# Scaling the third tile's finished rows in the last output stage, and splitting the last weight quarter three products sooner

## The chip, the core and the metric

The kernel runs on one NeuronCore of a Trainium2 chip. The metric is the device time of one execution in microseconds (us); a median over runs is given where there are several. Five engines appear in the profile: PE (TensorE, matrix products, with PEld for its weight loads), DVE (VectorE), ACT (ScalarE), POOL (GpSimd) and SP (SyncE, which here only issues DMAs). Each takes its own instructions strictly in the order in which they stand in the program, and waits where an instruction needs a result of another engine.

## The reference

Two layers on a residual stream x of 2048 rows by 1024 columns: a gated MLP with chunk-wise mixing, then attention of 64-row chunks to themselves and the 8 chunks before, with one key and value projection for all. What matters here is the end of it:

```python
def rms_norm(x, g):
    xf = x.astype(jnp.float32)
    y = xf * lax.rsqrt(jnp.mean(xf * xf, axis=-1, keepdims=True) + EPS)
    return (y * g.astype(jnp.float32)).astype(x.dtype)

def chunk_attention_mixer(h, k_pad, v_pad, w_qz, rel_bias, w_out):
    ...
    o = lax.map(one_chunk, (jnp.arange(n_chunks), q))      # softmax(q k + bias) v, 16 heads of 64
    return (o * jax.nn.silu(z)) @ w_out

x = x + chunk_attention_mixer(h, k_pad, v_pad, b_w_qz[i], b_rel_bias[i], b_w_out[i])
return rms_norm(x, final_norm_g)
```

## The kernel before

The attention layer works on four tiles of 512 rows (t = 0 to 3; the third tile is t = 2), and within a tile on eight pairs of heads (p = 0 to 7). A pair has eight score steps (two heads, four blocks of 128 queries). Beside these steps PE is given products of other work: the projections of the next pair, and the output projection of the tile before. In the last pair, t = 3 and p = 7, there is no next pair; there the rest of tile 2's output projection and the first 13 steps of tile 3's own stand beside the scores. What is left of tile 3's projection follows alone, and is called the last output stage here.

**Products.** Every product is taken in float32 accuracy by splitting both factors into a high and a low part of a faster type. The high part is a copy on ACT (L356 for the left factor, L1775 for a weight), the low part a subtraction on DVE (L361 `Qlo<-A_hh,Qho`, L1776 `wbo<-raw_bo,wbo`). Three matmuls (L111, L112, L113) multiply high by high, high by low, low by high; only the third needs the left factor's low part, only the second the weight's.

**The output projection** is one level of Strassen: seven products `ph` in the order 1, 7, 2, 6, 5, 4, 3, each for two halves `jp` of the rows. A product (ph, jp) is 4 groups of three matmuls, 12 in all. `last_all` (L1796) lists them for tile 3: `ltodo` holds the 14 pairs, so i = 5 is (2, 1), i = 7 is (6, 1) and i = 8 is (5, 0). In the second group of product i it splits the left factor of product i + 2 (`last_left`), and a table `plan` says which weights are fetched there (`last_right`). The weights of ph 1, 2 and 3 are plain quarters of the matrix that are fetched raw and split; the others were stored split. The quarter of ph 3, the last one, is fetched and split at i = 5.

**Evictions.** `o_evict` (L1819) adds each product into the rows: DVE reads PSUM and adds (L1927, L1932, L1941, L1949), POOL adds two tiles of SBUF (L1929, L1937, L1942, L1945). The first two products are copied by ACT. When a 128-row block is complete, ACT squares it (L1861) into a sum `ssq`, and `finish` (L1878) adds the two halves of the sum on DVE (L1881), adds epsilon (L125), takes the root on POOL (L126, 128x1), and `scale` multiplies the row by the root and the gain on DVE: two SCALAR_TENSOR_TENSOR of 128x512 at L1899. For tile 3 that comes at once. For tile 2 the finished sums go to DRAM (`x2d`), and `finish` fetches them back into a tile `y`, scales and sends them out.

**When tile 2's rows are finished.** The four `finish` calls of tile 2 (blocks 1, 3, 0, 2 in that order) are put on a list `finals`, each puts its `scale` in front of it, and something pops one entry at a time. Up to now two places do: the loop over the eight score steps (`if u and finals`, one entry per step), in the last pair as elsewhere, and `last_all`, once per product after i = 4. So blocks 1, 3 and 0 are scaled in the last pair, and block 2 in the last output stage.

**What sets the order.** The kernel is written in this order, and a planner of the tile framework then fixes one order per engine, from its own estimates and from tiles' data dependencies. `on_tick`, `on_beat` and `follow` add edges to that: an instruction may not be placed ahead of a named matmul (`tick`, `beat`) or instruction. Those edges set the order on one engine and cost no wait on the chip. A DMA is queued on SP in the order given; one that must wait, for its data or for a free buffer, holds all behind it.

## Time and profile before

| what | us |
|---|---|
| median of 3 runs (lowest and highest) | 2638.99 (2638.98 to 2643.34) |
| the profiled execution, its whole time | 2639.15 |
| its span, first to last instruction | 2637.2 |
| PE busy in the span | 2603.7 |
| DVE busy in the span | 1874.3 |
| POOL busy in the span | 884.6 |

Rows of a timeline hold the start, the duration, engine, line and operation with output and inputs, how many (x1), and in brackets the idle time of the engine just before with what ended it. Where several stand in one row (x2), the duration is that of all. A duration includes time in which the instruction, already issued, stands still; the next one often starts a little before it ends (0.60 us from start to start for a DVE row of 0.68). The view by stretches gives for each stretch the busy time of PE, PEld, DVE, ACT and POOL with the number of instructions, the granted PE clock as a share, the DMA engines' share and GB/s. The view of waits names who waited, for whom, the sum in us, how often, and the longest.

### The profile page before, as it was taken

To read this page: it belongs to the slowest core of one execution; us is meant where nothing else is said; L and a number is where in the kernel's file an instruction comes from. 1 tells how busy PE (TensorE), PEld (TensorE's weight loads), DVE (VectorE), ACT (ScalarE), POOL (GpSimd) and SP (SyncE) were. 2 spreads that over 40 slices of the span, in tenths; PEclk is the share of its full clock that TensorE was granted. 3 is DMA by queue.
4 is the path that set the end of the run, shared out by engine and by line. 5 is a ranking of instruction groups with operands and counts; after the bars stand their busy time and mean duration, and the time that the engine had idled before them with its cause. 6 is when DMAs were issued, how large, how long until landed. Compare 5 with 4: busy or idle time off the path is not lost. (4 is left out here: it accounts for less than half of the span.)

```text
span 2637.2 us, 38020 instructions
## 1 busy us (share of the span) xinstructions
PE 2603.7 (99%) x12976; PEld 2178.5 (83%) x12976; DVE 1874.3 (71%) x2942; ACT 1314.5 (50%) x2331; POOL 884.6 (34%) x871
## 2 busy tenths in 40 slices
PE   9999999999999999999999999999999999999997
PEld 7888888888888888888888878888888888888886
DVE  6655676866767667757776767777778777877677
ACT  5422243443433434343376566666656655666564
POOL 4611334143152322203233334344332322332245
PEclk9999999999999999999999999999999999999999
DMA  7899999999988869967886587778787666775677
GB/s 297 317 344 331 346 365 318 320 326 337 336 298 309 316 232 323 333 203 266 317 287 223 190 273 237 227 244 260 245 279 259 221 210 219 254 228 160 195 228 250
DMA packets 275153, 720.31 MB, mean 273 GB/s; under 512 B 28944, under 2 KB 68880, under 8 KB 274960
## 3 DMA queue, kind: packets, MB, share of 16 engines
q1 hardware_dynamic: 268096, 704.25, 77.8%
q10 hardware_dynamic: 6864, 13.63, 1.4%
q8 instruction: 104, 1.70, 0.3%
q14 instruction: 89, 0.73, 0.1%
HBM read 532.69 MB, written 174.59 MB: 268 GB/s over the span
## 5 line engine op out<-in xcount | busy, mean ns | idle before, releaser
L111 PE MATMUL P<-T,S 128*128 128x512 f32 x1248 | 495.1, 397 | 0.1
L113 PE MATMUL P<-T,S 128*128 128x512 f32 x1248 | 487.7, 391 | 0.0
L112 PE MATMUL P<-T,S 128*128 128x512 f32 x1248 | 487.3, 390 | 0.0
L1560 POOL TENSOR_SCALAR pr<-pr,sl 128x640 f32<-128x640 f32 (+4 forms) x256 | 205.9, 805 | 555.3 <-DVE sl L1559 469.0
L111 PE MATMUL pj<-hh_b,wh_b 128*128 128x512 f32 x768 | 319.0, 415 | 0.0
L113 PE MATMUL pj<-hh_b,wl_b 128*128 128x512 f32 x768 | 303.9, 396 | 0.3 <-DVE wl_b L242 0.3
L112 PE MATMUL pj<-hl_b,wh_b 128*128 128x512 f32 x768 | 302.3, 394 | 0.0
L1556 ACT ACTIVATE pr<-pr,nm 128x640 f32<-128x640 f32 (+4 forms) x256 | 195.5, 764 | 188.9 <-DVE nm L1549 187.2
L113 PEld LDWEIGHTS P<-T,S 128*128 128x128 f32 x1248 | 234.3, 188 | 50.7 <-DVE S L463 0.4
L112 PEld LDWEIGHTS P<-T,S 128*128 128x128 f32 x1248 | 235.0, 188 | 44.8 <-DVE T L463 0.5
L111 PEld LDWEIGHTS P<-T,S 128*128 128x128 f32 x1248 | 234.8, 188 | 44.9 <-DVE x L596 0.5
L1581 DVE TENSOR_TENSOR pt<-tp,pt 128x640 fp32r<-128x640 f32 (+4 forms) x256 | 188.6, 737 | 44.2 <-ACT pt L1580 41.5
L1549 DVE CUSTOM_DVE_ANT_0 pr<-s,bias 128x640 f32<-128x640 f32 (+4 forms) x256 | 188.1, 735 | 36.3 <-PE s L1541 29.8
L1580 ACT CAST pt<-tp 128x640 fp32r<-128x640 f32 (+4 forms) x256 | 158.7, 620 | 52.6 <-PE tp L1576 47.5
L1576 PE MATMUL tp<-ident,pr 128*128 128x128 f32 x1120 | 166.7, 275 | 11.0 <-DVE pt L1581 10.3
L113 PEld LDWEIGHTS pj<-hh_b,wl_b 128*128 128x128 f32 x768 | 144.2, 188 | 34.7 <-DVE wl_b L242 2.3
L1576 PEld LDWEIGHTS tp<-ident,pr 128*128 128x128 f32 x1120 | 130.7, 140 | 46.0 <-issue 15.4
L111 PEld LDWEIGHTS pj<-hh_b,wh_b 128*128 128x128 f32 x768 | 145.1, 189 | 17.4 <-ACT wh_b L241 1.2
L112 PEld LDWEIGHTS pj<-hl_b,wh_b 128*128 128x128 f32 x768 | 145.1, 189 | 16.6
L1601 PEld LDWEIGHTS pv<-pt,V 128*128 128x128 f32 x896 | 143.1, 188 | 18.4 <-DVE pt L1581 2.3
L1601 PE MATMUL pv<-pt,V 128*128 128x256 f32 (+3 forms) x896 | 153.8, 319 | 0.4 <-DVE pt L1581 0.4
L242 DVE TENSOR_TENSOR wl_b<-raw_b,wh_b 128x1024 fp32r<-128x1024 f32 x96 | 120.4, 1255 | 25.7 <-ACT wh_b L241 24.7
(307 smaller groups left out, 5723.6 us busy)
## 6 DMA issues: line engine op xcount, KB each, us to landing
S<-hsd SPq DMA_DIRECT2D x288, 512.0 KB, 5.5
rw<-in_w_a SPq DMA_DIRECT2D x108, 512.0 KB, 6.4
raw_b<-wk SPq DMA_DIRECT2D x75, 512.0 KB, 4.3
A<-ytd SPq DMA_DIRECT2D x72, 512.0 KB, 5.8
hsd<-S SPq DMA_DIRECT2D x56, 512.0 KB, 4.7
V<-vhd SPq DMA_DIRECT2D x56, 512.0 KB, 5.6
bias<-reld SPq DMA_DIRECT2D x64, 320.0 KB, 4.1
va<-vd SPq DMA_DIRECT2D x32, 512.0 KB, 6.0
```

The lines of the kernel that those rows point to most:

```text
L111: first = mm(ps, lh, rh, start=first, stop=False)
L112: mm(ps, lh, rl, start=False, stop=False)
L113: mm(ps, ll, rh, start=False, stop=last)
L242: tv(wl[:], raw[:], wh[:].bitcast(F32), op=sub)
L1549: nc.vector.tensor_tensor_reduce(out=pr[:, c0:].rearrange("p (a b) -> p a b", a=nseg), in0=ps[:, :nseg, :w], in1=bias[:, c0:].rearrange("p ...
L1556: nc.scalar.activation(pr[:, c0:], pr[:, c0:], AF.Exp, scale=-1.0, bias=nm[:], accum_out=sl[:])
L1560: nc.gpsimd.tensor_scalar(pr[:, c0:], pr[:, c0:], sl[:], 1.0, op0=ALU.mult, op1=ALU.mult)
L1576: ins = tpose(tp[:, b, :], pr[:, b * P : (b + 1) * P], ident[:])
L1580: nc.scalar.copy(oh, tp[:, b0:5, :].rearrange("p a b -> p (a b)"))
L1581: nc.vector.tensor_tensor(pt[:, 2560 + o + b0 * P : 2560 + o + 640], tp[:, b0:5, :].rearrange("p a b -> p (a b)"), oh.bitcast(F32), op=ALU ...
L1601: mm(po[:, q0 * P : q1 * P], vtl[t, p][:, i, hs], rhs, start=(i == blocks[0] and j == 0), stop=(i == 7 and j == 1),)
```

## The change

Four edits, all at the end of tile 3.

- The pops of `finals` by the score loop stop in the last pair (`t + 1 < NT or p + 1 < NPAIR`). In `last_all` they come in every second group of three matmuls (k = 1 and 3) after i = 4, in place of once per product. So all four blocks of tile 2 are finished and scaled in the last output stage: an entry at each of the eight places from (2, 1) to (6, 1) and (5, 0).
- Block 3 (b = 3) gets its own tile of two halves (tag C) in place of sharing the one tile `y` of tag bx with blocks 1 and 2.
- The fetch of the last weight quarter (ph = 3) stays listed at i = 5, while its split becomes a function `halves` that is listed at i = 7 for its first half and i = 8 for its second. A new argument `late` of `split_s` makes the left factor's split of (4, 0) follow the weight's, on ACT and on DVE, and the weight's split may not be placed ahead of the matmul named last (`on_tick`).
- Nothing is added to or left out of the arithmetic.

```diff
             ins = nc.scalar.copy(hi[:, ks], src[:, ks])
...
-            tv(lo[:, ks], src[:, ks], hi[:, ks].bitcast(F32), op=sub)
+            follow(ins, late[::2])
+            follow(tv(lo[:, ks], src[:, ks], hi[:, ks].bitcast(F32), op=sub), late[1::2])
...
+                late=late_w if (ph, jp) == (4, 0) else (),
...
-                nc.scalar.copy(w[0], raw[:])
-                tv(w[1], raw[:], w[0].bitcast(F32), op=sub)
+                def halves():
+                    hi = nc.scalar.copy(w[0], raw[:])
+                    lo = tv(w[1], raw[:], w[0].bitcast(F32), op=sub)
+                    if ph == 3:
+                        late_w.extend((on_tick(hi).ins.name, lo.ins.name))
+                if ph == 3:
+                    late_s.append(halves)
+                else:
+                    halves()
...
-                        if finals and i > 4:
-                            finals.pop(0)()
+                    if closed and i > 4 and k % 2 and finals:
+                        finals.pop(0)()
...
+                        if i in (7, 8):
+                            late_s.pop(0)()
...
-                elif t + 2 == NT and b == 0:
+                elif t + 2 == NT and b in (0, 3):
                     on_beat(first)
-                    y = [half_tile("og", f"y{t}_{b}_{c}", 2)[:] for c in range(2)]
+                    tag, n = ("C", 4) if b else ("og", 2)
+                    y = [half_tile(tag, f"y{t}_{b}_{c}", n)[:] for c in range(2)]
...
-                    if u and finals:
+                    if u and finals and (t + 1 < NT or p + 1 < NPAIR):
                         finals.pop(0)()
```

Nothing moves on any engine before the last pair. How the planner's order changes is shown at three places. In the names, `y2_3_0` is tile 2's row block 3, its first half; `Qlo_5_1` is the low part of the left factor of product (5, 1); `bo_6_0` is product (6, 0) in PSUM; `row1` and `ou3` are the rows and partial sums of tile 3; `pt3_15`, `pr3_15` and `s3_15` belong to the scores of head 15.

The first place is DVE in the middle of the last pair, at the last head's blocks. Before, from the split of (7, 0) on:

```order
L361 TENSOR_TENSOR Qlo_7_0_25429<-A_hl_25181,Qho_7_0_25428 128x512
L1621 TENSOR_TENSOR og32_3_7_25458<-pv3_14_25432,ot3_14_25459 64x512
L1581 TENSOR_TENSOR pt3_15_25449<-tp3_15_0_25450,pt3_15_25449 128x640
L1899 SCALAR_TENSOR_TENSOR y2_3_25375<-y2_3_25375,rr_f2_3_25371,gf_13667 128x512 x2
L1549 ISA pr3_15_3_25474,nm3_15_3_25475<-s3_15_3_25469,bias3_15_25125 128x640
L1549 ISA nm3_15_3_25475 128x1
L1581 TENSOR_TENSOR pt3_15_25449<-tp3_15_1_25490,pt3_15_25449 128x640
L1881 TENSOR_TENSOR rr_f2_0_25502<-ssq2_0_23968 128x1
L361 TENSOR_TENSOR Qlo_7_1_25520<-A_hl_25181,Qho_7_1_25519 128x512
L1559 RECIPROCAL sl3_15_3_25476<-sl3_15_3_25476 128x1
L125 TENSOR_SCALAR rr_f2_0_25502<-rr_f2_0_25502 128x1
L1899 SCALAR_TENSOR_TENSOR y2_0_0_25506<-y2_0_0_25506,rr_f2_0_25502,gf_13667 128x512
```

Now, from the same split on:

```order
L362 TENSOR_TENSOR Qlo_7_0_25411<-A_hl_25181,Qho_7_0_25410 128x512
L1622 TENSOR_TENSOR og32_3_7_25440<-pv3_14_25414,ot3_14_25441 64x512
L1550 ISA pr3_15_3_25456,nm3_15_3_25457<-s3_15_3_25451,bias3_15_25125 128x640
L1550 ISA nm3_15_3_25457 128x1
L1582 TENSOR_TENSOR pt3_15_25431<-tp3_15_0_25432,pt3_15_25431 128x640
L1560 RECIPROCAL sl3_15_3_25458<-sl3_15_3_25458 128x1
L362 TENSOR_TENSOR Qlo_7_1_25492<-A_hl_25181,Qho_7_1_25491 128x512
L1582 TENSOR_TENSOR pt3_15_25431<-tp3_15_1_25472,pt3_15_25431 128x640
L1781 TENSOR_TENSOR wlbo_2_1_25405<-raw_bo_2_1_25406,whbo_2_1_25404 128x1024
```

The scalings of blocks 3 and 0 and the small steps of their roots are gone from between the score steps; those of block 1, a little earlier, are gone as well.

The second place is DVE in the last output stage, at products (6, 0) to (4, 0). Before, from the eviction of (6, 0) on:

```order
L1941 TENSOR_TENSOR ou3_1_0_25484<-bo_6_0_25704,ou3_1_0_25484 128x512
L361 TENSOR_TENSOR Qlo_5_1_25734<-A_hl_25181,Qho_5_1_25733 128x512
L1941 TENSOR_TENSOR ou3_1_1_25529<-bo_6_1_25726,ou3_1_1_25529 128x512
L361 TENSOR_TENSOR Qlo_4_0_25754<-A_hh_25180,Qho_4_0_25753 128x512
L1927 TENSOR_TENSOR row1_25625<-bo_5_0_25746,row1_25625 128x512
L1932 TENSOR_TENSOR ou3_1_0_25484<-bo_5_0_25746,ou3_1_0_25484 128x512
L361 TENSOR_TENSOR Qlo_4_1_25778<-A_hh_25180,Qho_4_1_25777 128x512
```

Now, from the same eviction to the split of (4, 0):

```order
L1956 TENSOR_TENSOR ou3_1_0_25466<-bo_6_0_25668,ou3_1_0_25466 128x512
L1781 TENSOR_TENSOR wbo_3_0_25646<-raw_bo_3_0_25647,wbo_3_0_25646 128x1024
L362 TENSOR_TENSOR Qlo_5_1_25720<-A_hl_25181,Qho_5_1_25719 128x512
L1914 SCALAR_TENSOR_TENSOR y2_0_0_25713<-y2_0_0_25713,rr_f2_0_25709,gf_13667 128x512
L1956 TENSOR_TENSOR ou3_1_1_25501<-bo_6_1_25700,ou3_1_1_25501 128x512
L1914 SCALAR_TENSOR_TENSOR y2_3_0_25681<-y2_3_0_25681,rr_f2_3_25677,gf_13667 128x512
L1895 TENSOR_TENSOR rr_f2_2_25743<-ssq2_2_24023 128x1
L1914 SCALAR_TENSOR_TENSOR y2_3_1_25682<-y2_3_1_25682,rr_f2_3_25677,gf_13667 128x512
L125 TENSOR_SCALAR rr_f2_2_25743<-rr_f2_2_25743 128x1
L1781 TENSOR_TENSOR wbo_3_0_25646<-raw_bo_3_1_25649,wbo_3_0_25646 128x1024
L1914 SCALAR_TENSOR_TENSOR y2_0_1_25714<-y2_0_1_25714,rr_f2_0_25709,gf_13667 128x512
L362 TENSOR_TENSOR Qlo_4_0_25752<-A_hh_25180,Qho_4_0_25751 128x512
```

Six operations of two SBUF tiles now stand ahead of the low part of (4, 0): both halves of the weight split, and four halves of rows. After it come the eviction of (5, 0), the two halves of block 2 and `ou3_1_0`, and then `Qlo_4_1`. Block 1 takes the place that block 2 had, right behind `Qlo_6_1`.

The third place is POOL in the same stretch. Before, its sums follow each other:

```order
L1929 TENSOR_TENSOR row2_25558<-row2_25558,ou3_1_1_25529 128x512
L1942 TENSOR_TENSOR ou3_7_0_25586<-ou3_7_0_25586,ou3_1_0_25484 128x512
L1945 TENSOR_TENSOR row1_25625<-row1_25625,ou3_7_0_25586 128x512
L1937 TENSOR_TENSOR ou3_7_0_25586<-ou3_7_0_25586,row1_25625 128x512
L1942 TENSOR_TENSOR ou3_7_1_25639<-ou3_7_1_25639,ou3_1_1_25529 128x512
```

Now the roots of blocks 3 and 0 stand ahead of them:

```order
L1944 TENSOR_TENSOR row2_25528<-row2_25528,ou3_1_1_25501 128x512
L126 TENSOR_TENSOR rr_f2_3_25677<-rr_f2_3_25677,mhalf_179 128x1
L126 TENSOR_TENSOR rr_f2_0_25709<-rr_f2_0_25709,mhalf_179 128x1
L1957 TENSOR_TENSOR ou3_7_0_25548<-ou3_7_0_25548,ou3_1_0_25466 128x512
L1960 TENSOR_TENSOR row1_25587<-row1_25587,ou3_7_0_25548 128x512
L1952 TENSOR_TENSOR ou3_7_0_25548<-ou3_7_0_25548,row1_25587 128x512
L1957 TENSOR_TENSOR ou3_7_1_25601<-ou3_7_1_25601,ou3_1_1_25501 128x512
L1960 TENSOR_TENSOR row3_25589<-row3_25589,ou3_7_1_25601 128x512
L1952 TENSOR_TENSOR ou3_7_1_25601<-ou3_7_1_25601,row3_25589 128x512
L126 TENSOR_TENSOR rr_f2_2_25743<-rr_f2_2_25743,mhalf_179 128x1
```

The last two of its sums, `ou3_1_0` and `ou3_1_1`, follow there as before. On ACT both casts of the weight quarter now stand right behind the square of `row2` (product (2, 1)); the high part of (5, 1) lies between them and those of (4, 0) and (4, 1) follow. PE's order changes by a few places: among them, the first matmul of (4, 1) is placed ahead of the third of (4, 0), and the first of (3, 0) ahead of the third of (4, 1). On SP the fetches and stores of `y` for blocks 1, 3, 0 and 2 that stood between the weight fetches now stand behind the last of them, except the fetch of block 1.

## Prediction

> **What bounds the kernel now.** I read the page's busy shares first, then busy time by stretches over the end, then PE's waits there, then the timelines of DVE, POOL and PE. Nothing moves ahead of the last pair, so only the last 65 us count. From the page, and from the stretches (PE, PEld, DVE, ACT, POOL, the clock, the DMA share, GB/s) of the last pair and of the first part of the last output stage:

> ```profile
> PE 2603.7 (99%) x12976; PEld 2178.5 (83%) x12976; DVE 1874.3 (71%) x2942; ACT 1314.5 (50%) x2331; POOL 884.6 (34%) x871
> ```

> ```profile
> 2575.00:2598.00 23.00, 20.21 (x111) 16.46 (x110) 19.50 (x35) 13.18 (x25) 11.29 (x11) 1.00 0.91 306
> 2598.00:2620.00 22.00, 22.00 (x99) 18.18 (x98) 15.48 (x24) 9.53 (x21) 16.20 (x12) 1.00 0.74 283
> ```

> PE is the bound nearly everywhere, but in the last pair it stands for 2.8 us while DVE is busy 19.5 of 23 us. In the output stage PE never stands, DVE has 6.5 us to spare and POOL 5.8. Those two look free there; whether they are, the rest decides. PE's waits from 2574 to 2624, as a view gives them:

> ```profile
> PE tp L1576 <- DVE pt L1581: 2.4, 3, 1.1
> PE bo L112 <- DVE wbo L1776: 1.3, 2, 0.7
> PE s L1541 <- DVE nm L1549: 0.7, 1, 0.7
> PE tp L1576 <- DVE rr_f L1881: 0.3, 1, 0.3
> ```

> 2.4 + 0.7 + 0.3 = 3.4 us are score steps waiting for DVE in the last pair; 1.3 us is product (3, 0) waiting twice for the low half of its weight.

> **A. The scalings leave the last pair.** DVE's rows there:

> ```profile
> 2574.57 2.56 DVE L1899 SCALAR_TENSOR_TENSOR y<-y,rr_f,gf 128x512 f32<-128x512 f32 x2
> ...
> 2585.55 1.88 DVE L1899 SCALAR_TENSOR_TENSOR y<-y,rr_f,gf 128x512 f32<-128x512 f32 x2
> ...
> 2591.18 0.75 DVE L1899 SCALAR_TENSOR_TENSOR y<-y,rr_f,gf 128x512 f32<-128x512 f32 x1 [1.48 <-POOL rr_f L126]
> ...
> 2595.06 0.74 DVE L1899 SCALAR_TENSOR_TENSOR y<-y,rr_f,gf 128x512 f32<-128x512 f32 x1
> ```

> 2.56 + 1.88 + 0.75 + 0.74 = 5.9 us of DVE and 1.48 us of standing for POOL's root go. That is more than PE's 3.4 us of waits. I leave 0.6 of them, about one eviction, since an eviction and splits still stand between the score steps: **−2.8**, which is also what PE lacks in the stretch (23.00 − 20.21). Ends: −3.4 if all goes, −1.4 if only what the idle 1.48 us caused goes.

> **B. The weight's split comes sooner.** Around product (3, 0), and at the anchors that I need below, PE's rows are:

> ```profile
> 2612.48 0.39 PE L111 MATMUL bo<-wbo,Qho 128*128 128x512 f32 x1
> ...
> 2615.20 0.39 PE L111 MATMUL bo<-whbo,Qho 128*128 128x512 f32 x1
> ...
> 2620.64 0.39 PE L111 MATMUL bo<-wbo,Qho 128*128 128x512 f32 x1
> 2621.71 0.50 PE L112 MATMUL bo<-wbo,Qho 128*128 128x512 f32 x1 [0.69 <-DVE wbo L1776]
> ...
> 2627.69 0.39 PE L113 MATMUL bo<-wbo,Qlo 128*128 128x512 f32 x1
> ```

> Products (5, 1) and (4, 0) start 2.72 us apart, so a matmul takes 0.227. From 2620.64 to 2621.71 pass 1.07, so this wait cost 0.84 where the view says 0.69; 1.3 × 0.84 / 0.69 = 1.6. The split is now placed ahead of that of (4, 0), so **−1.6**. The last matmul, without these waits, would end at 2627.69 + 0.23 − 1.58 = 2626.34 (all times on the axis of before, A taken apart).

> **C. What the last stage now carries.** Six operations of two SBUF tiles stand on DVE ahead of the low part of (4, 0): two weight halves, four row halves. On POOL two roots come ahead of the sum of (6, 0). Whether DVE and POOL can do this side by side is seen where such operations meet. First POOL, then DVE (the last two fences start with the same instruction, alone and with its successor):

> ```profile
> 2609.45 1.30 POOL L1942 TENSOR_TENSOR ou<-ou,ou 128x512 f32<-128x512 f32 x1
> 2610.82 1.81 POOL L1945 TENSOR_TENSOR row<-row,ou 128x512 f32<-128x512 f32 x1
> ...
> 2618.82 1.75 POOL L1937 TENSOR_TENSOR ou<-ou,row 128x512 f32<-128x512 f32 x1
> 2620.54 2.27 POOL L1937 TENSOR_TENSOR ou<-ou,row 128x512 f32<-128x512 f32 x1
> ```

> ```profile
> 2611.40 0.68 DVE L1941 TENSOR_TENSOR ou<-bo,ou 128x512 f32<-128x512 f32 x1
> 2612.00 1.18 DVE L361 TENSOR_TENSOR Qlo<-A_hh,Qho 128x512 fp32r<-128x512 f32 x1
> ```

> ```profile
> 2619.95 1.71 DVE L1776 TENSOR_TENSOR wbo<-raw_bo,wbo 128x1024 fp32r<-128x1024 f32 x1
> ```

> ```profile
> 2619.95 3.94 DVE L1776 TENSOR_TENSOR wbo<-raw_bo,wbo 128x1024 fp32r<-128x1024 f32 x2
> ```

> They do not run together. POOL's second sum ends at 2620.57, the first weight half at 2621.66 (1.09 later), POOL's third sum at 2622.81 (1.15 later), the second weight half at 2623.89 (1.08 later). So they take strict turns, also where DVE has its next operation waiting, and hold 1.09 per weight half and 1.15 per sum. A low part beside a sum: 2613.18 − 2612.63 = 0.55; I take 0.57 for it and for a row half. The eviction at 2611.40, which reads PSUM, goes on in its 0.60 while the sum from 2610.82 runs.

> Now the turns. In before the sum of (6, 0) starts at 2609.45; two roots, 0.5 each (the stretch from 2632 below has one of 0.55), put it to 2610.45. From there to the end of the low part of (4, 0): POOL six sums, 6.9, and block 2's root, 0.5; DVE two weight halves, 2.2, and six operations of 0.57, 3.4; and the eviction of (6, 1), 0.6, in which POOL has nothing ready, as its next sum needs just that. 6.9 + 0.5 + 2.2 + 3.4 + 0.6 = 13.6, so 2624.05. The low part of (5, 1) is third behind the first weight half: 2610.45 + 1.15 + 1.15 + 1.09 + 1.15 + 0.57 = 2615.56.

> PE needs the latter at its third matmul, 2612.48 + 0.45 = 2612.93: a wait of **2.6**. (4, 0) then starts at 2617.8, and three matmuls later, at 2618.5, PE stands until 2624.05: **5.55**. The low part of (4, 1) follows an eviction, block 2's two halves and one more eviction: 2624.05 + 0.6 + 1.14 + 0.6 + 0.57 = 2626.96, where PE is ready at 2626.77: 0.2 (one matmul of (4, 1) was drawn ahead of the long wait). Behind it 33 matmuls are left, 7.5 us: last end 2634.45, against 2626.34: **+8.1**.

> Two inputs could make this worse. The cast of the first weight half on ACT stands behind the square of (2, 1)'s rows, and the quarter must have landed:

> ```profile
> 2609.52 0.63 ACT L1861 ACTIVATE jk<-row 128x512 f32<-128x512 f32 x1 [2.33 <-POOL row L1929]
> ```

> ```profile
> L1775 ACT CAST wbo<-raw_bo x2: 1032/1042/1052, 2618.9 to 2619.8; 128x1024 fp32r<-128x1024 f32 x2
> ```

> ```profile
> 2599.88 0.32 SPq L1779 DMA_DIRECT2D wlbo<-ows  x1
> ...
> 2602.46 1.61 SPq L1774 DMA_DIRECT2D raw_bo<-in_wb_out  x2
> ```

> ```profile
> raw_bo<-in_wb_out SPq DMA_DIRECT2D x2, 512.0 KB, 11.1
> ```

> The first half's fetch now stands where the row at 2599.88 stood; with 11.1 us it lands at 2611.0 and is cast by 2612.05, before its turn at 2612.75: no cost. Issued at 2602.46 as before, it would be cast at 2614.65; a sum of 1.15 would fill part of the gap, and 0.8 would remain. The fetches of blocks 3 and 0 now stand behind the weights and the store of block 1 on SP; if DVE has to wait for them, a sum on POOL takes its turn meanwhile, so I cost them at nothing.

> **The clock.** In the tail the granted clock shows what a long wait does:

> ```profile
> 2631.00:2632.00 1.00, 0.00 (x0) 0.00 (x0) 0.97 (x4) 0.18 (x2) 0.00 (x0) 0.89 0.08 29
> 2632.00:2633.00 1.00, 0.00 (x0) 0.00 (x0) 0.34 (x2) 0.00 (x0) 0.55 (x1) 0.50 0.99 365
> ```

> A mean of 0.89 means a fall to 0.50 at 2631.78, 3.7 us after the last matmul. In a wait from 2618.5 it would fall at 2622.2. No row shows when it returns. If after another 3.7 us, at 2625.9, then 1.85 us of work run at half: I take **+0.9**; ends 0 (the fall comes later) and 1.85 (3.7 us of work at half). [...]

> **D. The tail.** Its last scaling starts in before at

> ```profile
> 2632.76 1.41 DVE L1899 SCALAR_TENSOR_TENSOR row<-row,rr_f,gf 128x512 f32<-128x512 f32 x2 [0.66 <-POOL rr_f L126]
> ```

> and ends 6.25 us after the last matmul. The same chain hangs on (3, 1) afterwards: **0**.

> **The sum.** A −2.8, then +6.5 for the last matmul (C's 8.1 less B's 1.6), clock +0.9, D 0: +4.6. The profiled execution took 2639.15 (its span 2637.2), so 2643.75; the median of the runs is 0.16 lower: **2643.6**. No change means within 0.2%, 5.3 us, about what a measurement of this kernel can tell.

> **The rivals.** *The clock comes back late.* Half rate for 3.7 us of work costs 1.85, for two such stretches 3.7; the sum without the clock is +3.7, so +5.5 to +7.4, **2644.5 to 2646.4**: slower. It decides from the point where the wait is longer than 3.7 us and the clock still stands at 0.50 two microseconds after PE resumes. For it: the fall in the tail, and a wait of 5.55. Against: the fall may come late in the wait, and a shorter wait avoids it. Chance 0.25. [...]

> *DVE takes turn after turn* while it has work, and POOL comes in only where DVE does something else. The first weight half goes at 2612.75; DVE's own work from there to the low part of (4, 0) is 2.2 + 3.4 + 0.6 = 6.2, and two sums come in, at the eviction and at the tiny steps of a root: 2612.75 + 6.2 + 2.3 = 2621.25. The low part of (5, 1) is there at 2614.4. The waits are 1.5, 3.9 and, with a sum ahead of the low part of (4, 1), 1.3; less the matmul drawn ahead, 0.2, +6.5, and −4.4 + 6.5 = +2.1, with hardly a fall of the clock: **2641.1**. Against: the two weight halves with a sum between them. Chance 0.13.

> *The quarter lands late.* The first half of it costs 0.8 more, as above: **2644.4**. For it: 11.1 us from issue to landing, and only 0.7 in hand. Against: its place on SP. Chance 0.12.

> *The stage hides it.* If DVE's 6.5 us of spare time were all usable, as the shares suggest, C would be near 0: −2.8 − 1.6 = −4.4, **2634.6**. Against: every row above in which one of the two waits. Chance 0.06.

> *It does not do what it says*: the order shows the moved instructions; 0.01, 2638.8.

> **How the numbers follow.** Forecast 0.43, late clock 0.25, turn after turn 0.13, late quarter 0.12, hidden 0.06, nothing 0.01. The range leaves out the last two at its lower end, 2639.0, and reaches at its upper from 2646.4 by A's near end (+1.4) to 2648.0. Slower begins at 2644.3: most of the late clock (0.22), half of the late quarter (0.06), a quarter of the forecast (0.11): 0.39. Faster, below 2633.7, needs the hidden case with A at its far end, and a little more: 0.03. The rest, 0.58, is no change.

> **What would show it.** A: no wait of tp or s for DVE in the last pair. B: no wait for `wbo`. C: PE waits at L113 for `Qlo` in (5, 1) and (4, 0), together about 8 us, with DVE and POOL rows lengthened beside each other in turns; wrong if these waits stay below 4. Clock: a stretch at 0.50 inside the wait. The prediction falls if PE stays busy through (4, 0), or if the tail behind the last matmul changes by over a microsecond.

## The result and the profile after

| kernel | median, us | lowest to highest | runs |
|---|---|---|---|
| before | 2640.62 | 2636.32 to 2643.34 | 9 |
| changed | 2646.55 | 2643.81 to 2648.55 | 9 |

The ratio is 1.0021, with a 95% interval of 1.0012 to 1.0030: about 5.5 us slower, between 3.2 and 7.9. The interval leaves out a ratio of 1, so the kernel is slower; but the ratio stands on the bound of 0.2%, and whether the true one is over it, these runs leave open. The profiled execution took 2646.11 us, its span is 2643.9 (before 2639.15 and 2637.2). The forecast was 2643.6 and +4.6.

Executions differ by some microseconds before anything moved, so the stages are measured from one row of the last pair but one, ahead of all that the change touches (in the twelve profiles it starts between 2539.67 and 2544.57). It stands 1.43 us later in the profile of the changed kernel, and that much of the two spans' difference is not the change. Before, then after:

```profile
2540.21 2.66 PE L1601 MATMUL pv<-pt,V 128*128 128x512 f32 x16
```

```profile
2541.64 2.65 PE L1602 MATMUL pv<-pt,V 128*128 128x512 f32 x16
```

Product (5, 0) starts before the change at

```profile
2609.76 0.39 PE L111 MATMUL bo<-wbo,Qho 128*128 128x512 f32 x1
```

| from that row, us | to product (5, 0) | (5, 0) to the last matmul | last matmul to the last scaling | all |
|---|---|---|---|---|
| before | 69.55 | 17.93 | 5.07 | 92.55 |
| changed | 66.85 | 26.08 | 4.84 | 97.77 |
| difference | −2.70 | +8.15 | −0.23 | +5.22 |

The last scaling after the change, on DVE, is this:

```profile
2639.41 1.42 DVE L1914 SCALAR_TENSOR_TENSOR row<-row,rr_f,gf 128x512 f32<-128x512 f32 x2 [0.73 <-POOL rr_f L126]
```

The last pair gave 2.7 us, the last output stage took 8.15. PE's waits in the last pair (2575.43 to 2597.5) and then in the last output stage, after the change:

```profile
PE tp L1577 <- DVE pt L1582: 1.1, 3, 0.5
```

```profile
PE bo L113 <- DVE Qlo L362: 7.2, 2, 6.0
```

The first is what is left of 3.4 us. In the second, the wait for the weight's low half is gone, and two waits for low parts of the left factor have come. On PE they stand here (start, duration, and in brackets the wait):

```profile
2608.49 0.39 PE L111 MATMUL bo<-wbo,Qho 128*128 128x512 f32 x1
...
2611.44 0.39 PE L112 MATMUL bo<-wbo,Qho 128*128 128x512 f32 x1
2613.00 0.50 PE L113 MATMUL bo<-wbo,Qlo 128*128 128x512 f32 x1 [1.17 <-DVE Qlo L362]
...
2615.86 0.39 PE L111 MATMUL bo<-whbo,Qho 128*128 128x512 f32 x1
2622.23 0.80 PE L113 MATMUL bo<-whbo,Qlo 128*128 128x512 f32 x1 [5.99 <-DVE Qlo L362]
...
2627.07 0.40 PE L111 MATMUL bo<-wbo,Qho 128*128 128x512 f32 x1
...
2634.57 0.39 PE L113 MATMUL bo<-wbo,Qlo 128*128 128x512 f32 x1
```

The row at 2608.49 starts (5, 0), that at 2634.57 is the last matmul. From start to start, less the 0.227 of a matmul, PE loses 1.33 in (5, 1) and 6.14 in (4, 0).

What it waits for is seen by laying POOL beside DVE, from the sum of (6, 0) on:

```profile
2608.88 1.29 POOL L1957 TENSOR_TENSOR ou<-ou,ou 128x512 f32<-128x512 f32 x1
2610.25 2.15 POOL L1960 TENSOR_TENSOR row<-row,ou 128x512 f32<-128x512 f32 x1
2612.47 1.61 POOL L1952 TENSOR_TENSOR ou<-ou,row 128x512 f32<-128x512 f32 x1
```

```profile
2609.62 1.63 DVE L1781 TENSOR_TENSOR wbo<-raw_bo,wbo 128x1024 fp32r<-128x1024 f32 x1 [0.91 <-ACT wbo L1780]
2611.17 1.77 DVE L362 TENSOR_TENSOR Qlo<-A_hl,Qho 128x512 fp32r<-128x512 f32 x1
2612.86 1.77 DVE L1914 SCALAR_TENSOR_TENSOR y<-y,rr_f,gf 128x512 f32<-128x512 f32 x1
...
2615.82 1.22 DVE L1895 TENSOR_TENSOR rr_f<-ssq 128x1 f32<-128x1 f32 x1
...
2621.50 0.68 DVE L362 TENSOR_TENSOR Qlo<-A_hh,Qho 128x512 fp32r<-128x512 f32 x1
```

Take the ends (start plus duration) in order of time: sum 2610.17, weight half 2611.25, sum 2612.40, low part 2612.94, sum 2614.08, scaling 2614.63. Each ends 0.54 to 1.15 after the one before, which is on the other engine. From the first weight half on, a duration is the instruction's own work plus what is left of the neighbour's: the two take turns. From 2608.88 the chain runs 13.3 us, to the end of the low part of (4, 0) at 2622.18, and PE resumes at 2622.23.

Busy time of PE, PEld, DVE, ACT and POOL, the clock and the DMA from (5, 0) to the last matmul, before and after:

```profile
2609.80:2627.90 18.10, 16.84 (x73) 13.13 (x71) 14.04 (x21) 8.13 (x18) 13.63 (x10) 1.00 0.29 108
```

```profile
2608.50:2634.80 26.30, 19.15 (x73) 14.80 (x71) 23.05 (x31) 8.23 (x19) 16.31 (x12) 0.87 0.39 133
```

PE's 73 matmuls are the same. The ten further DVE instructions make it busy for 9.0 us more, and the DVE time that looked free before was partly POOL's turn. The clock's mean of 0.87 is a fall inside the wait, seen in stretches of 0.2 us:

```profile
2620.00:2620.20 0.20, 0.00 (x0) 0.00 (x0) 0.20 (x1) 0.00 (x0) 0.20 (x1) 1.00 0.01 0
2620.20:2620.40 0.20, 0.00 (x0) 0.00 (x0) 0.20 (x1) 0.00 (x0) 0.20 (x1) 0.53 0.00 0
...
2626.80:2627.00 0.20, 0.20 (x2) 0.20 (x1) 0.20 (x1) 0.20 (x1) 0.20 (x1) 0.50 0.29 82
2627.00:2627.20 0.20, 0.20 (x2) 0.13 (x1) 0.20 (x2) 0.20 (x1) 0.20 (x1) 0.91 0.00 0
```

A mean of 0.53 in a stretch of 0.2 us that began at 1.00 puts the fall to 0.50 at 2620.21, 4.1 us after PE stopped (2615.86 + 0.23); the mean of 0.91 puts the return at 2627.04, 6.83 us later. From 2622.23 to 2627.07 PE does 11 matmuls in 4.84 us in place of 11 × 0.227 = 2.50.

### The profile page after: what moved, and what is told of

Read it like the earlier page. It is cut to its first block, busy times and chain, and to the rows that moved or that the text cites. A ratio compares the mean times of both kernels' runs of the same rounds, so it can differ in the third digit from the quotient of the medians.

```text
span 2643.9 us, 38031 instructions
## 1 busy us (share of the span) xinstructions
PE 2606.5 (99%) x12976; PEld 2180.7 (82%) x12976; DVE 1875.7 (71%) x2942; ACT 1313.8 (50%) x2331; POOL 884.9 (33%) x871
## 5 line engine op out<-in xcount | busy, mean ns | idle before, releaser
L111 PE MATMUL P<-T,S 128*128 128x512 f32 x1248 | 495.8, 397 | 0.0
L113 PE MATMUL P<-T,S 128*128 128x512 f32 x1248 | 488.1, 391 | 0.1
L112 PE MATMUL P<-T,S 128*128 128x512 f32 x1248 | 487.6, 391 | 0.3 <-DVE T L464 0.3
L111 PE MATMUL pj<-hh_b,wh_b 128*128 128x512 f32 x768 | 318.8, 415 | 0.0
L113 PE MATMUL pj<-hh_b,wl_b 128*128 128x512 f32 x768 | 304.0, 396 | 0.3 <-DVE wl_b L242 0.2
L112 PE MATMUL pj<-hl_b,wh_b 128*128 128x512 f32 x768 | 302.4, 394 | 0.0
L113 PEld LDWEIGHTS P<-T,S 128*128 128x128 f32 x1248 | 234.6, 188 | 51.1 <-DVE S L464 0.4
L112 PEld LDWEIGHTS P<-T,S 128*128 128x128 f32 x1248 | 235.4, 189 | 45.0 <-DVE T L464 0.6
L111 PEld LDWEIGHTS P<-T,S 128*128 128x128 f32 x1248 | 235.2, 188 | 44.7 <-DVE lmv L673 0.2
L1581 ACT CAST pt<-tp 128x640 fp32r<-128x640 f32 (+4 forms) x256 | 158.7, 620 | 51.2 <-PE tp L1577 46.4
L113 PEld LDWEIGHTS pj<-hh_b,wl_b 128*128 128x128 f32 x768 | 144.2, 188 | 34.6 <-DVE wl_b L242 2.3
L111 PEld LDWEIGHTS pj<-hh_b,wh_b 128*128 128x128 f32 x768 | 145.1, 189 | 17.4 <-ACT wh_b L241 1.2
L112 PEld LDWEIGHTS pj<-hl_b,wh_b 128*128 128x128 f32 x768 | 145.1, 189 | 16.6
## 6 DMA issues: line engine op xcount, KB each, us to landing
S<-hsd SPq DMA_DIRECT2D x288, 512.0 KB, 5.3
rw<-in_w_a SPq DMA_DIRECT2D x108, 512.0 KB, 6.3
raw_b<-wk SPq DMA_DIRECT2D x75, 512.0 KB, 4.2
A<-ytd SPq DMA_DIRECT2D x72, 512.0 KB, 5.8
hsd<-S SPq DMA_DIRECT2D x56, 512.0 KB, 4.7
V<-vhd SPq DMA_DIRECT2D x56, 512.0 KB, 6.0
va<-vd SPq DMA_DIRECT2D x32, 512.0 KB, 5.7
```

The costliest lines, as they stand in the source:

```text
L111: first = mm(ps, lh, rh, start=first, stop=False)
L112: mm(ps, lh, rl, start=False, stop=False)
L113: mm(ps, ll, rh, start=False, stop=last)
L1581: nc.scalar.copy(oh, tp[:, b0:5, :].rearrange("p a b -> p (a b)"))
```

## The experiments

The theory: the two engines take turns, and the low parts of (5, 1) and (4, 0) stand behind six operations that must take them. Its rivals: the scalings and the split cost nothing there, and something else holds PE; or the clock, not the wait, is most of the loss. In each result the first number is the change in us by the trace against before, measured as above (one profile of each; the part up to (5, 0) read 69.50 to 69.55 in the three kernels that leave the last pair as it was, and 66.3 to 67.2 in the nine others); the ratio is of timed runs, with its 95% interval.

**The split alone.** All that belongs to the scalings is undone, the split of the quarter stays three products sooner.

```diff
-                    if closed and i > 4 and k % 2 and finals:
-                        finals.pop(0)()
+                        if finals and i > 4:
+                            finals.pop(0)()
...
-                    if u and finals and (t + 1 < NT or p + 1 < NPAIR):
+                    if u and finals:
```

> The other part of the change alone: the scalings stay in the last pair and once per product, the weight's split is listed at (6, 1) and (5, 0), and (4, 0)'s left factor is still split behind it. The planner puts both casts and both halves behind the evictions of (5, 1), and the left factor of (4, 0) behind them, on ACT and on DVE. So PE stands after (5, 1), which ends at 2615.2 on before's axis: two evictions, two casts (to 2618.4), the left factor's cast (2618.9), two weight halves with sums of POOL between, the low part of (4, 0) at about 2622: 6.3 us of waiting, a fall of the clock, and B's -1.6 gained: +5 to +7 us against before. Rival (the early split by itself is a gain of 1.6 and only the scalings cost): -1.6.

Measured: +7.5; ratio 1.0029 (1.0019 to 1.0040). PE waits 5.2 us for ACT and 1.0 for DVE:

```profile
PE bo L111 <- ACT Qho L356: 5.2, 1, 5.2
PE bo L113 <- DVE Qlo L362: 1.0, 1, 1.0
```

With the scalings back in the last pair, the high part of (4, 0) stands on ACT behind both casts of the weight, and those behind the eviction of (5, 1), which itself waits for a sum on POOL:

```profile
2620.94 0.69 DVE L1941 TENSOR_TENSOR row<-bo,row 128x512 f32<-128x512 f32 x1 [2.60 <-POOL row L1959]
```

```profile
2622.29 1.98 ACT L1780 CAST wbo<-raw_bo 128x1024 fp32r<-128x1024 f32 x2
2624.17 1.13 ACT L356 CAST Qho<-A_hh 128x512 fp32r<-128x512 f32 x2
```

The time is 0.5 over the upper end expected. The split alone costs at least as much as the two parts together, so the parts do not add: what PE waits for is whichever low or high part stands behind the moved work.

**The scalings alone.** The split goes back to i = 5.

```diff
-                late=late_w if (ph, jp) == (4, 0) else (),
...
-                if ph == 3:
-                    late_s.append(halves)
-                else:
-                    halves()
+                halves()
...
-                        if i in (7, 8):
-                            late_s.pop(0)()
```

> One part of the change alone: all four blocks scaled in the last output stage, the last weight quarter split where it is fetched. The planner then puts the cast and the split of the first weight half into (2, 1) already, ahead of block 1's scaling, and the second one place sooner than in the changed kernel. Turns theory: one weight half and one turn fewer between the sum of (6, 0) and the low part of (4, 0), so PE waits about 4.0 there in place of 6.0, but up to 1 us somewhere in (6, 1) or (2, 1), where ACT now stands for the landing of the first half; clock as in the changed kernel or a little better: +2.5 to +4 us against before. Rival (the early split alone is to blame and the scalings cost nothing): -2.7, the gain of the last pair, remains.

Measured: +5.0; ratio 1.0022 (1.0013 to 1.0031). One wait, where two were expected:

```profile
2620.67 0.80 PE L113 MATMUL bo<-whbo,Qlo 128*128 128x512 f32 x1 [7.13 <-DVE Qlo L362]
```

The rival that scalings cost nothing falls. The expected wait of 4.0 us falls too. The chain is shorter, 12.1 us (2608.53 to 2620.6), as it should be with a weight half out of it. But its first sum starts 0.7 later against (5, 0), and PE reaches (4, 0) 1.4 sooner, since it has not waited in (5, 1). In both kernels the chain on DVE and POOL gives PE one date. What PE saves ahead of it, it waits there.

**The split later.** The scalings are back in the last pair, as in the split alone; the split comes at i = 8 and 9, behind the low parts. Against the split alone, cut:

```diff
-                late=late_w if (ph, jp) == (4, 0) else (),
...
-                        if i in (7, 8):
+                        if i in (8, 9):
                             late_s.pop(0)()
```

> Before, with the weight's split listed at (5, 0) and (5, 1), and without the rule that (4, 0)'s left factor comes behind it; the scalings as before. DVE then has the low parts of (4, 0), (4, 1) and (3, 0) ahead of the two weight halves, which follow the eviction of (4, 0): about 1.3 us sooner than before, with POOL's last sums beside them as before. PE's waits for the weight shrink from 1.6 to between 0 and 0.9: -0.7 to -1.6 us. If the weight halves are held by POOL's sums as long as before, 0.

Measured: 0.0; ratio 0.9995 (0.9986 to 1.0004). The weight's low half is again PE's only wait, 1.3 us, and DVE shows why:

```profile
2621.35 0.68 DVE L1962 TENSOR_TENSOR row<-bo,ou 128x512 f32<-128x512 f32 x1
2621.96 3.94 DVE L1780 TENSOR_TENSOR wbo<-raw_bo,wbo 128x1024 fp32r<-128x1024 f32 x2
```

The two halves stand behind the eviction of (4, 0), as before the change, and take 3.94 us with POOL's sums between them, to the hundredth what they took before. My expectation took them to come 1.3 us sooner than before; they start 10.20 us after (5, 0), before 10.19. The earlier listing has left DVE's order here as it was, and the time with it; the listing costs only where it puts the halves ahead of what PE needs, as in the split alone.

**No sums on POOL.** The eight sums of products 5 and 6 on POOL are left out, so tile 3's rows lack them (the expectation speaks of ten; eight it is). DVE's work is unchanged.

```diff
-                                tg(y, y, place(r, c, jp) if last else rows.pop(0), op=add)
+                                if not last:
+                                    tg(y, y, rows.pop(0), op=add)
...
-                    tg(y_, y_, x_, op=add)
-                    if last:
-                        c = place(1, 1, jp)
-                        tg(c, c, y_, op=add)
+                    if not last:
+                        tg(y_, y_, x_, op=add)
```

> The changed kernel without POOL's ten sums of products 6 and 5 of the last tile (so its rows lack them); DVE keeps its order word for word. Turns theory (POOL's sums and DVE's operations of two SBUF tiles hold each other off): DVE runs through alone; the low part of (4, 0) is there at about 2616.0 on the changed kernel's axis in place of 2622.2, PE waits 1.4 us there and not at all in (5, 1), in place of 7.2 in all, the clock does not fall: 5.8 + 2.0 less, about -2 us against before. Rival (DVE's own queue is what is long, POOL runs beside it): the waits stay at 7 us and the time at +5.5.

Measured: −0.5; ratio 0.9993 (0.9984 to 1.0002). PE's wait is 1.8 us, where 7.2 was and 1.4 was expected. DVE's rows stand without a partner:

```profile
2612.67 1.23 DVE L1781 TENSOR_TENSOR wbo<-raw_bo,wbo 128x1024 fp32r<-128x1024 f32 x1 [0.90 <-DMA out<-y]
2613.82 0.68 DVE L362 TENSOR_TENSOR Qlo<-A_hl,Qho 128x512 fp32r<-128x512 f32 x1
2614.42 0.74 DVE L1914 SCALAR_TENSOR_TENSOR y<-y,rr_f,gf 128x512 f32<-128x512 f32 x1
```

The weight half takes 1.23 us against 1.63 above, low part and scaling 0.68 and 0.74 against 1.77 each. So POOL's sums make most of the wait; the 1.8 that is left is DVE's own queue. The time is 1.5 over what was expected, since the clock falls here too (for 3.41 us, from 2620.56), which was not expected. The run takes POOL's work away altogether, and doesn't yet show that the turns are for two operands in SBUF; the next one bears on that.

**The gain in PSUM.** ACT copies the gain once to PSUM, and the scalings read it there. DVE and POOL have the same work, and one operand of the scalings lies elsewhere. The order on DVE is not quite that of the changed kernel: the planner puts the four halves of blocks 3 and 0 together, behind the second weight half.

```diff
+                if i == 5:
+                    gain.append(pss.tile([P, 2, 512], F32, tag="ss", name="gain"))
+                    nc.scalar.copy(
+                        gain[0][:].rearrange("p a b -> p (a b)"), gf[:]
+                    )
...
-                            y[c], y[c], r[:], gf[:, cs], op0=ALU.mult, op1=ALU.mult
+                            y[c], y[c], r[:], gain[0][:, c, :] if gain else gf[:, cs],
+                            op0=ALU.mult, op1=ALU.mult,
```

> The changed kernel, with the gain copied once by ACT into two free PSUM banks ahead of the last output stage; tile 2's scalings read it from there, so that they have one SBUF tile as input in place of two. Same work on DVE and POOL; the planner puts the four halves of blocks 3 and 0 behind the second weight half instead of around it. Turns theory: the scalings take no turns any more; the low part of (5, 1) waits as before, 1.3, that of (4, 0) is there after about 2.2 us of waiting in place of 6.0, and the clock does not fall: 3.7 + 2.0 less than the changed kernel, about -0.2 us against before. Rival (DVE's own queue): as many operations of the same length stand ahead of the low part of (4, 0), the time stays at +5.5. Rival (rows or weights land late): also +5.5.

Measured: +1.1; ratio 1.0008 (0.9999 to 1.0017). PE's waits and the scalings on DVE:

```profile
PE bo L113 <- DVE Qlo L362: 4.2, 2, 3.7
```

```profile
2614.75 2.71 DVE L1920 SCALAR_TENSOR_TENSOR y<-y,rr_f,gain 128x512 f32<-128x512 f32 x4
```

```profile
2615.21 1.26 POOL L1967 TENSOR_TENSOR row<-row,ou 128x512 f32<-128x512 f32 x1
2616.55 1.26 POOL L1959 TENSOR_TENSOR ou<-ou,row 128x512 f32<-128x512 f32 x1
```

Four halves in 2.71 us, 0.68 each, while two of POOL's sums go on beside them, each in 1.26: neither is lengthened, so these scalings take no turns. The waits fell by 3.0 us, to 4.2 where 3.5 was expected; how much of that is the new order, this run does not separate. Not expected was that the longest wait is still 3.7 us and that the clock falls at its end, for 3.41 us, from 2618.41 to 2621.82:

```profile
2618.40:2618.60 0.20, 0.18 (x1) 0.18 (x2) 0.20 (x1) 0.00 (x0) 0.00 (x0) 0.53 1.16 420
...
2621.80:2622.00 0.20, 0.20 (x2) 0.16 (x2) 0.20 (x1) 0.00 (x0) 0.20 (x1) 0.94 0.00 0
```

**PE kept at work in the wait.** Ahead of the third matmul of (4, 0), 26 matmuls into a spare PSUM tile are added, so that PE does not stand. This separates the clock from the wait.

```diff
-                    ins = mm3(ps[:], *vs[k], hi[:, c], lo[:, c], k == 0, k == 3)
+                    if (ph, jp, k) == (4, 0, 0):
...
+                        for j in range(26):
+                            d = follow(
+                                mm(fill[:], vs[0][0], hi[:, c], start=j == 0, stop=j == 25),
+                                [d.ins.name],
+                            )
+                        ins = mm(ps[:], vs[0][1], hi[:, c], start=False, stop=False)
+                        follow(ins, [d.ins.name])
+                    else:
+                        ins = mm3(ps[:], *vs[k], hi[:, c], lo[:, c], k == 0, k == 3)
```

> The changed kernel, with 26 more matmuls of 128x512 put on PE between the second and the third matmul of (4, 0); they write a PSUM tile that nobody reads. 26 x 0.227 = 5.9 us lie inside the 6.0 us that PE stood there. All other engines keep the order of the changed kernel. If the fall of the clock costs what I read from the trace (11 matmuls from 2622.23 to 2627.07, 4.84 us in place of 2.50, so 2.3 less the 0.3 that PE would then wait for the low part of (4, 1)), the clock stays at 1.00 and the kernel is 2.0 us faster than the changed one: about +3.5 us against before. If DVE is late behind the wait anyhow, so that the clock costs nothing, the time stays that of the changed kernel, +5.5, and PE waits over 2 us more behind (4, 0).

Measured: +6.3; ratio 1.0026 (1.0013 to 1.0038).

```profile
2617.59 6.05 PE L1830 MATMUL fill<-whbo,Qho 128*128 128x512 f32 x26
2624.04 0.50 PE L1833 MATMUL bo<-whbo,Qlo 128*128 128x512 f32 x1 [0.40 <-DVE Qlo L362]
```

The granted clock stays at 1.00 until the tail, and the stage takes 24.95 in place of 26.08: the fall costs 1.13 net. That is less than the 2.34 (4.84 − 2.50) that PE loses in it. At full speed PE comes too soon to (4, 1) and (3, 0), where single matmuls start up to 0.27 us later than their turn. But part of the difference is order and not clock: the changed kernel does the first matmul of (4, 1) inside the wait, this one behind it (0.23), and here ACT casts the high part of (3, 0) one square later, which makes its low part late (0.27). So the price of the fall lies between 1.1 and 2.3 of the 8.15 us that the stage lost, and the rival that the clock is most of the loss falls. But the tail grew from 4.84 to 7.58. With the fill the planner put the small steps of blocks 3 and 0 of tile 3 elsewhere, so the total says nothing of the clock.

**The same with the tail held.** The finishing of a block of tile 3 is put behind the next product's eviction.

```diff
                     if last:
-                        finish(b)
+                        pend.append(b)
+                        if (r, c, jp) == (0, 1, 1):
+                            finish(pend.pop(0))
...
+                if ev is not None:
+                    follow(first, [ev.ins.name])
...
-                    tv(o, ps, y, op=add)
+                    ev = tv(o, ps, y, op=add)
+                    while pend:
+                        finish(pend.pop(0), ev)
```

> The run fill again (26 more matmuls inside PE's wait), with edges that keep DVE's order behind the last matmuls of (4, 0) to (3, 1) as in the changed kernel: the small steps and the scaling of a finished block stand behind the next product's eviction. The clock stays at 1.00 as in fill, so from (5, 0) to the last matmul again about 25 us, and the tail is back from 7.6 to about 4.9 us: 2.7 less than fill and about 1.1 less than the changed kernel, +4.0 to +4.6 us against before. That 1.1 is what the fall of the clock cost. If the longer tail of fill had another cause than DVE's order, it stays, and with it +6 to +7.

Measured: +4.8; ratio 1.0016 (1.0007 to 1.0025). The stage takes 24.92, as in the run before, so the 1.1 to 1.2 by which the stage shortens is seen twice. The tail takes 6.03, not 4.84: 1.5 of the 2.7 us came back. In the rest, the first block's scaling starts 2.24 us ahead of the last matmul where it was 3.18, and from it to the last scaling pass 8.27 in place of 8.02; ACT's order is not that of the changed kernel here either. The stage is 1.16 shorter and the tail 1.19 longer, so what the fall costs at the kernel's end these two runs leave open.

**Low parts first.** This tries to keep the gain of the last pair without its price. The gain lies in PSUM. The weight's halves are listed at i = 8 and 9 behind the low part listed last; each pair of scalings is listed at a place of its own and likewise follows the newest low part. Against the changed kernel, cut:

```diff
+            if tag == "Q":
+                newest[:] = [lo_.ins.name]
...
+                        on_tick(hi)
+                        follow(lo, newest)
...
+                        if i in (8, 9):
+                            late_s.pop(0)()
+                    if (i, k) in ((5, 3), (6, 3), (8, 1), (10, 3)):
+                        scales.pop(0)()
...
+                            if t + 2 == NT:
+                                follow(ins, newest)
```

> A version that should beat both: all four blocks scaled in the last stage as in the changed kernel, from a gain in PSUM (no turns with POOL), block 2 in a tile of its own, and on DVE the low part of (4, 0) ahead of the first weight half, that of (4, 1) ahead of the second, block 2's scaling behind the low part of (3, 0). Turns theory: PE waits under 1 us for the low part of (4, 1) and about 1 us for that of (3, 0) in place of 7.2 in all, the clock does not fall, the last pair's 2.7 us stay gained: -1 to -2.5 us against before. Rival (any move of the scalings into the last stage makes DVE late there): PE waits 4 us or more, +2 or slower.

Measured: −1.8; ratio 0.9992 (0.9984 to 1.0001). The last pair keeps 3.2 us of gain, the stage takes 18.38 where 17.93 was; PE's waits are down to 1.7, and the clock stays at 1.00 until the tail. The tail is 0.9 longer.

**The same with the gain in SBUF.** One operand goes back, nothing else.

```diff
-                            y[c], y[c], r[:], gain[0][:, c, :] if gain else gf[:, cs],
+                            y[c], y[c], r[:], gf[:, cs],
```

> The same as low_parts_first but for one operand: the scalings read the gain from SBUF, so that each takes turns with POOL's sums. Same order on DVE up to the low part of (3, 1). Turns theory: ahead of the low part of (4, 0) two halves, ahead of that of (4, 1) two more, each with up to one sum of 1.15 us: PE waits 3 to 5 us longer than with the gain in PSUM, +1 to +3 us against before. Rival (what reads the gain from where does not matter): same time as low_parts_first.

Measured: +4.3; ratio 1.0013 (1.0004 to 1.0022). The stage takes 23.46, and PE waits 4.4. One pair of scalings in the two kernels:

```profile
2611.66 1.41 DVE L1931 SCALAR_TENSOR_TENSOR y<-y,rr_f,gain 128x512 f32<-128x512 f32 x2
```

```profile
2611.48 2.90 DVE L1931 SCALAR_TENSOR_TENSOR y<-y,rr_f,gf 128x512 f32<-128x512 f32 x2
```

The order of the two is the same, and 1.41 us have become 2.90. By medians the two kernels are 5.6 us apart (2640.33 and 2645.90), by the trace 6.1. The +4.3 is over the +1 to +3 expected, though the wait of 4.4 us is only 2.7 longer than the two waits of low parts first: it brings a fall of the clock, for 6.83 us:

```profile
2621.60:2621.80 0.20, 0.00 (x0) 0.00 (x0) 0.20 (x2) 0.00 (x0) 0.00 (x0) 0.70 0.02 0
...
2628.40:2628.60 0.20, 0.20 (x2) 0.20 (x1) 0.20 (x1) 0.00 (x0) 0.20 (x1) 0.73 0.00 0
```

PE's first 11 matmuls behind the wait take 4.86 us in place of 2.50, so of the 5.1 by which the stage is longer, about half is the longer wait and half the clock. The changed kernel and low parts first are 7.0 us apart by the trace: the new order takes 0.9 of that (5.2 to 4.3), the place of one operand 6.1. So the turns, with the fall of the clock that they bring, are most of what the change costs.

**The tail reordered.** Low parts first, with the finishing held as above, and the scaling of block 3 of tile 3 behind the eviction of (3, 1).

```diff
-                if last:
+                if last and b == 3:
+                    held_scale.append(scale)
+                elif last:
+                    if b == 0:
+                        held_scale.pop(0)(ev)
                     scale()
```

> low_parts_first, with the scaling of row block 3 placed behind the eviction of the last product, (3, 1), by an edge; in low_parts_first two blocks' scalings, 2.7 us, stand ahead of it. The eviction then starts about 1.3 us sooner, the last root is ready while block 3 and 0 are scaled, and the tail behind the last matmul's start shrinks from 6.0 to about 4.7: -2.5 to -3.5 us against before. If the end hangs on stores, not on DVE, the time stays that of low_parts_first.

Measured: −2.4; ratio 0.9993 (0.9984 to 1.0001), median 2639.48 against 2641.79 of the kernel before. The tail is 5.31, where 4.7 was expected. By the trace it is the fastest version found, by the ratio it is level with low parts first; the interval holds no change, so it is not shown to beat before.

## Why the prediction was right, point by point

**A, −2.8: −2.70.** The rule by which it was taken (all of PE's waits there, less about one eviction) held. The waits that are left, 1.1, are more than the 0.6 allowed, so about 0.4 of the gain lies outside them; the trace gives it no name.

**B: right.** No wait for the weight's low half is left in the changed kernel.

**C, two waits of 2.6 and 5.55: 1.33 and 6.14.** The mechanism was right, the first wait was half as long. The step that was off is the date of the first weight half: it was taken to wait until 2612.75 on the axis of before, a turn later, for two sums to come first. On record stands that the fetch takes the place of the row at 2599.88; after the change it was issued sooner, and the cast came sooner:

```profile
2594.24 0.83 SPq L1777 DMA_DIRECT2D raw_bo<-in_wb_out  x1
```

```profile
2608.55 1.04 ACT L1780 CAST wbo<-raw_bo 128x1024 fp32r<-128x1024 f32 x1
```

Ready at 2609.6, the half went right behind the first sum, and the low part of (5, 1) was there 4.45 us after the start of (5, 0), where 5.80 had been worked out. The low part of (4, 0) was there after 13.69 where 14.29 had been: the chain of six sums on POOL and eight operations on DVE was 13.3 for 13.6, and began 0.3 sooner, since the two roots held the first sum back by 0.7 and not by 1.0. PE, having waited 1.3 less, stood the longer there. The third wait, 0.2 at (4, 1), does not show.

**The clock, +0.9: between 1.1 and 2.3.** The fall was placed 3.7 us after PE stops and the return 3.7 after the fall, so that 1.85 us of work would run at half rate. The fall came after 4.1, but the return 6.83 after the fall, 4.8 after PE resumed. So the step that was off is the length of the spell, 6.83 us where 3.7 was taken. That length was the author's estimate, taken over from the time to the fall, and no run shows a spell of 3.7 us (measured were 3.41, 6.83 and 10.24). What PE loses, 2.34, is over the upper end of 1.85 that was given; in the run with the fill, without a fall, the stage was 1.13 shorter. That the fall came near 3.7 is luck in part: in the split alone it came 2.6 us after PE stopped.

**D, 0: −0.23.**

**The sum, +4.6: +5.2 by the trace, 5.5 by the timed ratio.** The stage: +8.15 where +6.5 and +0.9 make 7.4. The two waits are 7.47 for 8.15, 0.7 less, and the clock's raw loss 2.34 for 0.9, 1.4 more: the 0.75 between. So two terms were mis-sized in opposite directions, the clock and C's first wait, and that the sum came out so near is in part luck. The rivals: *hidden* falls by the waits of 7.2, *turn after turn* by the six ends above, which alternate, *the quarter lands late* by the cast at 2608.55. *The clock comes back late* is what happened to the clock: the wait was longer than 3.7 us, it still stood at 0.50 more than two microseconds after PE resumed, and the loss of 2.34 lies within this rival's 1.85 to 3.7. PE worked in only 4.8 of the 6.8 us, and in the run with the fill the stage is shorter by 1.13 and not by 2.34. The measured median lies just above the span given for it (2644.5 to 2646.4); by the trace, which takes off the 1.43 us that came before the change, the total lies between the forecast and it.

## What to carry to other kernels

DVE's and POOL's idle shares could not be added up here where both worked on SBUF tiles: 9.0 us more of busy DVE went with 8.15 more of the stage. Look in the trace for two neighbours whose ends alternate, and price each instruction at its own hold plus one of the other engine's (of the low part's 1.77 us above, 0.54 was its own and 1.15 the sum's). Work moved off a busy stage into an idle-looking one should be listed behind what the bound engine needs next, or have one operand moved from SBUF to PSUM (1.41 us for a pair of scalings, 2.90 with that operand in SBUF); here the two together took the loss away, though a gain over before is not shown. And where one chain on other engines sets a date for the bound engine, shortening a wait ahead of that date lengthens the wait at it.

## What the runs showed of the hardware

**Turns.** Between the back-to-back DVE instructions with two SBUF inputs above, POOL's next sum came in each time: the six ends alternate, 0.54 to 1.15 us apart. A tiny step was lengthened too: the 128x1 addition at 2615.82, beside POOL's sum from 2615.37 to 2617.03, took 1.22 us, where one in a quiet stretch of the run with the fill took 0.16:

```profile
2631.62 0.16 DVE L1907 TENSOR_TENSOR rr_f<-ssq 128x1 f32<-128x1 f32 x1 [0.19 <-ACT jk L1887]
```

With the gain in PSUM, the scalings took no turn: 0.68 for a half, beside POOL's sums of 1.26.

| run | clock falls | PE resumes | clock returns | spell, us |
|---|---|---|---|---|
| no sums | 2620.56 | 2619.67 | 2623.97 | 3.41 |
| gain in PSUM | 2618.41 | 2618.42 | 2621.82 | 3.41 |
| changed | 2620.21 | 2622.23 | 2627.04 | 6.83 |
| low parts first, gain in SBUF | 2621.68 | 2623.52 | 2628.51 | 6.83 |
| scalings alone | 2616.42 | 2620.67 | 2626.66 | 10.24 |
| split alone | 2622.08 | 2624.84, and once more 2627.46 | 2632.32 | 10.24 |

Counted in steps of 3.41 us from the fall, each of the six ended with the first step in which PE worked throughout (with the gain in PSUM, but for 0.01 us). In the changed kernel PE resumed 2.0 us into the first step, and the clock returned at the end of the second: that is the length which the prediction missed. The scalings alone, from fall to return:

```profile
2616.40:2616.60 0.20, 0.00 (x0) 0.00 (x0) 0.20 (x2) 0.00 (x0) 0.20 (x1) 0.55 0.00 0
...
2626.60:2626.80 0.20, 0.20 (x2) 0.17 (x2) 0.20 (x1) 0.08 (x1) 0.20 (x1) 0.85 0.00 0
```

The standing ahead of a fall differed. In the changed kernel PE had stood for 4.1 us when the clock fell; without sums PE stood for only 1.80 us, and the clock fell at 2620.56, when PE was at work again:

```profile
2619.67 0.50 PE L113 MATMUL bo<-whbo,Qlo 128*128 128x512 f32 x1 [1.80 <-DVE Qlo L362]
```

```profile
2620.40:2620.60 0.20, 0.20 (x3) 0.16 (x2) 0.20 (x1) 0.20 (x1) 0.00 (x0) 0.90 1.01 389
```

Of the 3.41 us ahead of that fall PE stood for 1.80. Waits of 0.67 and 1.02 us (low parts first) brought no fall. How long PE must stand for one was not settled.
